# Hybrid encoder layer: side work stepped on every second step, attention as a pipeline of one burst each, all values in front

## The chip, the cores and the metric

One NeuronCore of a Trainium2 chip runs the whole program. The metric is device microseconds from start to end of one execution; the number for a kernel is the median of its runs.

## The reference

One step of a hybrid encoder trunk with one layer, for 512 prompt tokens and 8 sequences of 16 new tokens each, side by side as T = 640 columns. Model width is 2048, all in fp32. Cut to what matters:

```
z = x @ w_in              # q,k,v,f,gate of FoX | q,k,v,a,beta,gate of the delta rule | two merge gates
# branch A, 8 heads: forgetting attention
p = softmax(q k^T * scale + c_q - c_k, causal);  o_a = p @ v      # c: running sum of log-forget
#   prompt: 4 blocks of 128 queries; decode: 16 new queries per sequence over 512 cached rows and themselves
y_a = (o_a * silu(gate_a)) @ w_out_fox
# branch B, 8 heads: gated delta rule
q,k,v = silu(conv4(qkv));  q,k normalised
for chunk n:  v_new = u - w S;  o = q S + (q k^T * decay) v_new;  S = S * g + k_tail^T v_new
y_b = (rms_norm(o) * silu(gate_b)) @ w_out_gdn
h  = (sig(m_a) * y_a + sig(m_b) * y_b) @ w_out
x1 = LayerNorm(alpha * x + h);  out = x1 + sig(x1 @ w_pl_gate) * RMSNorm(p @ w_pl_proj)
```

Keys, values, log-forgets, the conv's last rows and the delta states are outputs too.

## The kernel before, in words

**Main work.** Every fp32 operand of the large products is split into two halves, high and low, and each product is three matmuls (hi·hi, hi·lo, lo·hi). x stays in SBUF as 16 tiles of 128 x 640 and the weights stream through. A *column* is one output block of 128 features: 16 steps, each of six matmuls 128x320 (`mm6`, L303 to L308; a step is thus "six column matmuls"). `pair` (L360 to L401) makes two columns with fewer products (L382). `wide` (L336 to L358) makes the 1024 values of FoX in two groups of 512 features: five row tiles, each a PSUM bank of 512, all five fed by 16 steps (L351). Its five banks are four of tag "g" and one of tag "o". When a row tile is done, `fin` in `values` copies its bank to a temporary in SBUF (ScalarE for even tiles, VectorE for odd) and sends it out by two DMAs: to `vd`, from where the heads read it back, and to the output `out_fv`. There are two temporaries, used in turn, so a copy waits for the two DMAs of the copy before last.

**Stages.** `front` runs the first FoX columns, values group 0 with a sum of x tiles (`sums`) beside it, then 14 pairs. `phase_fox` runs the q and k columns of heads 1 to 7, values group 1 behind head 3, then three merge-gate columns (`mcol`) and two projections. `phase_gdn` runs four columns for each of 8 delta heads (in the order q, k, v, gate) with a merge-gate column behind each, then the output columns. `tail` ends the layer.

**Side work.** Attention and delta rule are generators on *lanes*. After each step of a column, `tick` (L108) lets each lane take one stage of its generator if its wake time has come and, unless the lane is marked dry, if `banks_free` says that the PSUM banks of the next stages will have been read (by a running estimate of costs, `watch`, `clock` and `busy`). What a stage gives to TensorE stands in its queue between two steps of the column; I call it a *burst*. `par` (L129) takes two generators together, the decode part `fox_dec` and the prompt part `fox_pro`. The engines run in program order, so a burst whose input is late holds up the columns behind it. Side work takes PSUM banks from `sps`, tag "s", three banks in the FoX phase and four in the delta phase.

**One FoX head** (`fox`, L575). Prompt, for each block i of queries: scores (`mm3`, L299 to L301; block 0 is one fp32 matmul) into a bank, VectorE adds bias and mask, softmax (max L566, exp L568, scale L570 and L571), transposes of the probabilities (L704, one for each 128 keys), a copy to SBUF (`pT`, ScalarE, L706), output matmuls (L713) and a product with the gate (`og`, L715). Scores of block i+1, transposes of i and output of i are separate bursts. Decode: scores against the cache by 8 matmuls on quarter arrays, 128x32, 512 columns wide (L616) into bank `s1`, its softmax over 640 in `xd`, five transposes (L638, L645), copies `ppad` (L640) and `pn`, then 32 quarter-array matmuls of 128 columns against the cached values (L659) into bank `od`, in four bursts of 8; then a transpose and the store of `og`. A head's k and v caches (four pieces each, 512 KB), its values (`vn`, read back from `vd`) and its bias are loaded by SyncE's DMA queue, which the weight pieces (`wr`) share.

**Weights.** `w_ahead` (L257) issues one load ahead; a piece is then cast to its high half (`wh`, ScalarE, L253) and the low half is the difference (`wl`, VectorE, L254).

Of the kernel before, what the change touches and what calls it, by code (L numbers as in the profile page):

```python
# [9 lines left out]
F32 = mybir.dt.float32  # L10
# [4 lines left out]
ALU = mybir.AluOpType  # L15
# [32 lines left out]
class Kernel:  # L48
# [9 lines left out]
    PAIR0, PAIRS = 6, 4 + FRONT // 2  # L58
# [4 lines left out]
    def __init__(self, tc, ins, outs):  # L63
        self.clock, self.busy, self.paced = 0.0, [0.0, 0.0], False
        self.tc, self.nc, self.i, self.o = tc, tc.nc, ins, outs
        self.lanes = []
        self.banks, self.read, self.nbanks = [], {}, 3
        self.now = 0
# [60 lines left out]
    def par(self, *gens):  # L129

        live = [[g, 0, 0.0] for g in gens]
        t = 0
        while live:
            for e in list(live):
                if e[1] <= t and e[2] <= self.clock:
                    try:
                        n, e[2] = self.watch(e[0])
                        e[1] = t + n
                    except StopIteration:
                        live.remove(e)  # L140
            if live:
                yield self.FREE
                t += 1
# [398 lines left out]
    def values_of(self, h):  # L542

        while self.vdone <= h // 4:
            yield 1
        if h not in self.vn:
            self.vn[h], self.vat = self.zt([P, 5, P], "vn", 2), self.now
            self.nc.sync.dma_start(out=self.vn[h], in_=self.vd[:, :, h * P:(h + 1) * P].rearrange("t p d -> p t d"))
            return
        while self.now < self.vat + 6:  # L550
            yield 1
# [9 lines left out]
    def softmax(self, xs, n):  # L561


        nc = self.nc
        nm = self.zt([P, 1], "nm", 3)
        nc.vector.reduce_max(out=nm, in_=xs[:, 0:n], axis=AX.X, negate=True)  # L566
        sm = self.zt([P, 1], "sm", 3)
        nc.scalar.activation(xs[:, 0:n], xs[:, 0:n], AF.Exp, bias=nm, accum_out=sm)  # L568
        yield 2
        nc.vector.reciprocal(sm, sm)  # L570
        nc.vector.tensor_scalar(out=xs[:, 0:n], in0=xs[:, 0:n], scalar1=sm, scalar2=0.5, op0=ALU.mult,  # L571
                                op1=ALU.mult)
        yield 1
# [35 lines left out]
    def fox_dec(self, h, q, k, sg, og):  # L609
        nc = self.nc  # L610
        nb, nbd = self.bias[h]
        s1 = self.sps()
# [19 lines left out]
        yield 1  # L632
# [10 lines left out]
        yield 1  # L643
# [4 lines left out]
        yield 2  # L648
        yield from self.values_of(h)
        yield from self.values_of(h)  # L650
        vn = self.vn[h]
        od = self.sps()
        nc.tensor.matmul(od[:, 0:P], pn, vn[:, 4, :], start=True, stop=False, skip_group_check=True)
        for par in range(2):
            for c in range(4):
# [5 lines left out]
                if c == 1:  # L661
                    yield
# [4 lines left out]
        on = self.zt([P, P], "sq", 2, "on")  # L667
        nc.scalar.copy(out=on, in_=od[:, 0:P])
        yield 2
# [3 lines left out]
        pt = self.sps()  # L673
        nc.tensor.transpose(pt[:, 0:P], on, self.ident)
        nc.vector.tensor_tensor(out=og[:, NPT:T], in0=pt[:, 0:P], in1=sg[:, NPT:T], op=ALU.mult)
        yield 2

    def fox_pro(self, h, q, k, qp, kp, sg, og):
# [16 lines left out]
        xs = scores(0)  # L695
        yield 2
        for i in range(4):
            w = P * (i + 1)
            yield from self.softmax(xs, w)
            nx = scores(i + 1) if i < 3 else None  # L700
            yield 2
            pt = self.sps()
            for kb in range(i + 1):
                nc.tensor.transpose(pt[:, kb * P:(kb + 1) * P], xs[:, kb * P:(kb + 1) * P], self.ident)  # L704
            pT = self.zt([P, NPT], "pT")
            nc.scalar.copy(out=pT[:, 0:w], in_=pt[:, 0:w])  # L706
            yield 2
            yield from self.values_of(h)
            yield from self.values_of(h)
# [5 lines left out]
            nc.vector.tensor_tensor(out=og[:, i * P:w], in0=ops[:, 0:P], in1=sg[:, i * P:w], op=ALU.mult)  # L715
            xs = nx
# [54 lines left out]
    def gdn(self, h, kq, v):  # L771
# [5 lines left out]
        junk = self.zt([P, P], "junk")  # L777
        kt = self.zt([P, 5, P], "kt", 2)
        vr = self.zt([P, 5, P], "vr", 2)
        pk = self.sps()  # L780
        for t in range(4):
            nc.tensor.transpose(pk[:, t * P:(t + 1) * P], kq[:, 0, t * P:(t + 1) * P], self.ident)
        nc.scalar.copy(out=kt[:, 0:4, :], in_=pk.rearrange("p (a b) -> p a b", b=P))
        yield
        pd = self.sps()
        nc.tensor.transpose(pd[:, 0:P], kq[:, 0, NPT:T], self.ident)
        nc.tensor.transpose(pd[:, P:2 * P], v[:, NPT:T], self.ident)
        nc.tensor.transpose(pd[:, 2 * P:3 * P], kq[:, 1, NPT:T], self.ident)
        nc.scalar.copy(out=kt[:, 4, :], in_=pd[:, 0:P])
        nc.scalar.copy(out=vr[:, 4, :], in_=pd[:, P:2 * P])  # L790
        nc.scalar.activation(junk, pd[:, 2 * P:3 * P], AF.Square, accum_out=ss[:, 9:10])
        yield
        for t in range(5):
            nc.scalar.activation(junk, kt[:, t, :], AF.Square, accum_out=ss[:, t:t + 1])
        yield
        pq = self.sps()
        for t in range(4):
            nc.tensor.transpose(pq[:, t * P:(t + 1) * P], kq[:, 1, t * P:(t + 1) * P], self.ident)
        for t in range(4):
            nc.scalar.activation(junk, pq[:, t * P:(t + 1) * P], AF.Square, accum_out=ss[:, 5 + t:6 + t])  # L800
        yield
        pv = self.sps()
        for t in range(4):
            nc.tensor.transpose(pv[:, t * P:(t + 1) * P], v[:, t * P:(t + 1) * P], self.ident)
        nc.scalar.copy(out=vr[:, 0:4, :], in_=pv.rearrange("p (a b) -> p a b", b=P))
# [278 lines left out]
    def run(self, ctx):  # L1084
# [25 lines left out]
        self.blocks, self.chunks = self.lane(), self.lane()  # L1110
# [19 lines left out]
    def values(self, g, temp, after=None):  # L1130
# [11 lines left out]
        self.wide([self.gps(512) for _ in range(4)] + [self.ps2.tile([P, 512], F32, tag="o", name="o", bufs=1)],  # L1142
                  fin, after)
        self.vdone = g + 1

    def front(self, work):
# [4 lines left out]
        self.vdone = 0  # L1151
# [20 lines left out]
        wu = self.ps2.tile([P, 512], F32, tag="o", name="wu", bufs=1)  # L1172
# [70 lines left out]
        self.values(0, lambda t: self.spare[t % 2], lambda s: sums(s // 2) if s % 2 else None)  # L1243
# [46 lines left out]
    def phase_fox(self, work):  # L1290
# [5 lines left out]
        self.foxdone = -1  # L1296
# [6 lines left out]
        for h in range(H):  # L1303
# [16 lines left out]
            if h == 3:  # L1320
                self.values(1, lambda t: self.zt([P, T], ("sc", "eacc")[t % 2], 1, "vt"))
# [33 lines left out]
    def phase_gdn(self, conv, work):  # L1355
# [13 lines left out]
        for h in range(H):  # L1369
            for c in range(4):  # L1370
                acc = self.column()[0]
                kq = self.kqs[h % 2]
                if c == 2:
                    v = self.zt([P, T], "v")
                self.until(lambda: self.untapped == 0)
                if c == 3:
                    sg = self.zt([P, T], "sg")
                    self.silu_evac(acc, sg, "cth")
                    nc.sync.dma_start(out=self.sgd[h], in_=sg)
                else:  # L1380
                    ct = 8 * c + h
                    self.untapped += 1
                    stp = self.strip_evac(acc, ct)
                    conv["gens"].append(self.conv_silu(stp, ct, h if c == 1 else 0, v if c == 2 else kq[:, 1 - c, :]))
# [68 lines left out]
    def e_evac(self, n, ps):  # L1453

        nc = self.nc
        if n == 0:
            self.until(lambda: not self.work["gens"])
# [280 lines left out]
def _layout(a):  # L1738
# [15 lines left out]
    bl += [bq[0], bk[0], *bv[0]]  # L1754
# [3 lines left out]
    for h in range(1, H):  # L1758
        bl += [bq[h], bk[h], *(bv[1] if h == 3 else [])]
# [4 lines left out]
    for h in range(H):  # L1764
        bl += [gq[h], gk[h], gv[h], gg[h]]
        if h < 7:
            bl += m[nf + 3 + r * h:nf + 3 + r * (h + 1)]
# [72 lines left out]
```

## Time and profile before

| | us |
| --- | --- |
| median of 3 runs | 2252.88 (2249.75 to 2255.94) |
| the profiled execution | 2256.83 |
| its span | 2255.0 |

The profiled execution lies 3.95 us above the median, and 1.8 us of its time lie around the span. TensorE is busy 99% of the span. Rows of the timeline give start, duration, engine, line and operation; in brackets is the idle time of the engine ahead of the row and what ended it. Several equal instructions in a row are one row; a matmul of fp32 shows as two records, so "x16" on such a row is 8 matmuls. The recorded duration of a matmul overlaps the next one's, so costs on TensorE are taken from starts.

### The profile page before, as it was taken

Reading aid. Unit: us, or ns where it says so; the run is one execution under the profiler, and the core shown is the slowest. Engines: PE = TensorE matmul, PEld = TensorE weight load, DVE = VectorE, ACT = ScalarE, POOL = GpSimd, SP = SyncE. Lnnn points to the kernel's source line nnn. Section 1 sums busy time; section 2 is a strip of 40 time slices with the busy share of each in tenths; the row PEclk is TensorE's granted clock in tenths of the full one; section 3 lists DMA queues with packets and bytes.
Section 4 is the critical chain, followed back from the end, with each engine's and each line's share of the span. In section 5 each row is a group of like instructions: output and inputs, shape, how many; then the busy total and the mean of one; then the engine's idle time right before and its main releaser. Section 6 shows DMA issues by size and latency. Waiting matters only on the chain.

```text
span 2255.0 us, 39956 instructions
## 1 busy us (share of the span) xinstructions
PE 2240.8 (99%) x15938; PEld 2154.1 (96%) x15938; DVE 1328.8 (59%) x2831; ACT 842.7 (37%) x1874; POOL 68.3 (3%) x230
## 2 busy tenths in 40 slices
PE   9999999999999999999999999999999999999999
PEld 7899999988799999999999999999999999999999
DVE  5867666633434345476776776776537533667555
ACT  4444443423233335443543543544332212243222
POOL 0000000000000000000001000000000000020000
PEclk9999999999999999999999999999999999999999
DMA  6333332466555555223333323335447532323332
GB/s 226 124 117 104 122 118 99 134 223 212 198 191 191 179 171 172 93 85 101 106 101 101 109 92 98 119 103 174 161 156 234 174 99 99 99 98 108 122 122 69
DMA packets 118378, 304.56 MB, mean 135 GB/s; under 512 B 22680, under 2 KB 30952, under 8 KB 118192
## 3 DMA queue, kind: packets, MB, share of 16 engines
q1 hardware_dynamic: 118192, 302.01, 40.1%
q8 instruction: 125, 2.05, 0.4%
q14 instruction: 61, 0.50, 0.1%
HBM read 250.15 MB, written 51.82 MB: 134 GB/s over the span
## 4 chain that ended last, share of the span: by engine, by line
PE 95%; DVE 2%; DMA 2%; ACT 1%; issue 0%; SPq 0%; ACTq 0%; DVEq 0%
PE g L307 34%; PE g L308 33%; PE g L382 15%; PE g L351 3%; PE s L659 1%; PE s L713 1%; PE s L616 1%; PE o L351 1%; PE s L852 1%; DMA wr<-in_w 0%; PE s L989 0%; PE s L704 0%; DMA kc<-in_kc 0%; DVE wl L254 0%; DVE xr L1231 0%
## 5 line engine op out<-in xcount | busy, mean ns | idle before, releaser
L254 DVE TENSOR_TENSOR wl<-wr,wh 128x512 fp32r<-128x512 f32 x556 | 380.8, 690 | 523.5 <-ACT wh L253 496.9
L307 PE MATMUL g<-xh,wh 128*128 128x320 f32 (+1 forms) x1712 | 555.7, 325 | 0.6 <-ACT wh L253 0.4
L253 ACT CAST wh<-wr 128x512 fp32r<-128x512 f32 x556 | 341.1, 619 | 511.4 <-PE g L308 427.9
L307 PE MATMUL g<-xl,wh 128*128 128x320 f32 (+1 forms) x1712 | 530.0, 310 | 0.3 <-DVE xl L282 0.3
L308 PE MATMUL g<-xh,wh 128*128 128x320 f32 x1712 | 529.6, 309 | 0.0
L307 PE MATMUL g<-xh,wl 128*128 128x320 f32 (+1 forms) x1712 | 529.2, 309 | 0.0
L308 PE MATMUL g<-xl,wh 128*128 128x320 f32 x1712 | 529.1, 309 | 0.0
L308 PE MATMUL g<-xh,wl 128*128 128x320 f32 x1712 | 528.9, 309 | 0.0
L307 PEld LDWEIGHTS g<-xh,wh 128*128 128x128 f32 x1712 | 323.0, 189 | 17.6 <-issue 12.7
L308 PEld LDWEIGHTS g<-xh,wh 128*128 128x128 f32 x1712 | 323.0, 189 | 0.7
L307 PEld LDWEIGHTS g<-xl,wh 128*128 128x128 f32 x1712 | 322.8, 189 | 0.7 <-DVE xl L282 0.7
L308 PEld LDWEIGHTS g<-xl,wh 128*128 128x128 f32 x1712 | 322.6, 188 | 0.0
L307 PEld LDWEIGHTS g<-xh,wl 128*128 128x128 f32 x1712 | 322.0, 188 | 0.1
L308 PEld LDWEIGHTS g<-xh,wl 128*128 128x128 f32 x1712 | 321.8, 188 | 0.0
L382 PE MATMUL g<-xh,wh 128*128 128x320 f32 x448 | 138.6, 309 | 1.1 <-ACT u L392 1.1
L382 PE MATMUL g<-xh,wl 128*128 128x320 f32 x448 | 138.6, 309 | 0.0
L382 PE MATMUL g<-xl,wh 128*128 128x320 f32 x448 | 138.5, 309 | 0.0
L254 DVE TENSOR_TENSOR wl<-sr,wh 128x512 fp32r<-128x512 f32 x112 | 75.7, 690 | 62.3 <-ACT wh L253 62.0
L253 ACT CAST wh<-sr 128x512 fp32r<-128x512 f32 x112 | 67.8, 617 | 68.2 <-PE g L382 68.2
L382 PEld LDWEIGHTS g<-xh,wh 128*128 128x128 f32 x448 | 84.2, 188 | 1.4 <-ACT u L392 1.4
L382 PEld LDWEIGHTS g<-xh,wl 128*128 128x128 f32 x448 | 84.3, 188 | 0.0
L382 PEld LDWEIGHTS g<-xl,wh 128*128 128x128 f32 x448 | 84.1, 188 | 0.0
(388 smaller groups left out, 2921.2 us busy)
## 6 DMA issues: line engine op xcount, KB each, us to landing
wr<-in_w SPq DMA_DIRECT2D x276, 512.0 KB, 3.6
kc<-in_kc SPq DMA_DIRECT2D x32, 512.0 KB, 5.2
vc<-in_vc SPq DMA_DIRECT2D x32, 512.0 KB, 4.1
xr<-in_xT SPq DMA_DIRECT2D x32, 320.0 KB, 3.9
md<-m SPq DMA_DIRECT2D x32, 320.0 KB, 2.5
sab<-md SPq DMA_DIRECT2D x32, 320.0 KB, 3.5
sr<-in_w SPq DMA_DIRECT2D x14, 512.0 KB, 4.4
ed<-e SPq DMA_DIRECT2D x16, 320.0 KB, 3.7
```

Of the source, the lines that this page charges most:

```text
L253: nc.scalar.copy(out=hi, in_=src)
L254: nc.vector.tensor_tensor(out=lo, in0=src, in1=hi.bitcast(F32), op=ALU.subtract)
L307: nc.tensor.matmul(ps[0], whl[w], xhl[o][:, a], start=(first and x == 0), stop=(last and x == 2))
L308: nc.tensor.matmul(ps[1], whl[w], xhl[o][:, b], start=(first and x == 0), stop=(last and x == 2))
L351: nc.tensor.matmul(ps, x[:, sl], w, start=(s == 0 and n == 0), stop=(s == 15 and n == 2))
L382: nc.tensor.matmul(ps, a[:, w], b, start=(k == 0 and n == 0 and not more), stop=(k == 7 and n == 2), skip_group_check=True)
L616: nc.tensor.matmul(s1[32 * j:32 * j + 32, :], self.qpad[:, 2 * j + par, :], kc[:, (j % 2) * NPT:(j % 2 + 1) * NPT], start=(par == 0), stop ...
L659: nc.tensor.matmul(od[32 * j:32 * j + 32, 0:P], self.ppad[:, c, 2 * j + par, :], vc[:, o:o + P], start=False, stop=(par == 1 and c == 3), ...
L713: nc.tensor.matmul(ops[:, 0:P], vn[:, kb, :], pT[:, kb * P:(kb + 1) * P], start=(kb == 0), stop=(kb == i))
L852: nc.tensor.matmul(pp[:, o:o + 256].rearrange("p (a b) -> p a b", a=2), hl[w][:, 0, x], hl[m][:, :, x], start=(n == 0), stop=(n == 2))
```

## The change

Nothing is computed that was not computed before; instructions change places, and banks.

- Lanes that are not dry step on every second tick (`every` = 2; 1 from delta head 7 on). The lane `blocks` is now dry. `par` counts ticks.
- A new bank tag "d" with one bank (`dps`) takes the place of "o"; it holds `s1`, `od` and the wide's fifth row tile.
- Values: both groups run in `front`, one behind the other; `sums` goes with the second. `values_of` is gone: `load_v` reads a head's values back when the head starts.
- `fox_pro` is a pipeline: one burst holds the output of block i-2, the transposes of block i-1 and the scores of block i+1, and softmax i follows. `fox_dec` gives its quarter-array output matmuls in two bursts of 16 in place of four of 8, and its five transposes in one. The bias of the next head is loaded inside `fox_dec`, behind the head's last scores. The last transpose and the store of `og` go to the lane `ends` (`fox_out`).
- Delta rule: order of columns q, v, k, gate; the 15 transposes at a head's start go in two bursts (7 and 8) in place of four.

The diff, cut to its core:

```diff
     def tick(self):
         self.now += 1
         for q in self.lanes:
-            if q["gens"] and q["wake"] <= self.now and q["t"] <= self.clock and (q["dry"] or self.banks_free()):
+            if q["gens"] and q["wake"] <= self.now and q["t"] <= self.clock and (
+                    q["dry"] or not self.paced or (self.now % self.every == 0 and self.banks_free())):
                 self.step(q)
...
+    def dps(self):
+        return self.ps2.tile([P, 512], F32, tag="d", name="s", bufs=1)
...
     def fox(self, h, q, k):
-        if self.vdone > h // 4:
-            yield from self.values_of(h)
+        self.load_v(h)
...
-        og = self.zt([P, T], "og")
-        yield from self.par(self.fox_dec(h, q, k, sg, og), self.fox_pro(h, q, k, qp, kp, sg, og))
-        if h + 1 < H:
-            self.load_bias(h + 1)
-        nc.sync.dma_start(out=self.ogd[h], in_=og)
-        yield
+        yield from self.par(self.fox_dec(h, q, k), self.fox_pro(h, q, k, qp, kp, sg))
+        self.ends["gens"].append(self.fox_out(h, sg))
...
     def fox_dec
-        s1 = self.sps()
+        s1 = self.dps()
...
-        yield 1
         pt = self.sps()
         nc.tensor.transpose(pt[:, 0:P], xd[:, NPT:T], self.ident)
         pn = self.zt([P, P], "sq", 2, "pn")
         nc.scalar.copy(out=pn, in_=pt[:, 0:P])
-        yield 2
-        yield from self.values_of(h)
-        yield from self.values_of(h)
+        yield 4
+        while self.scored < h:
+            yield 2
+        if h + 1 < H:
+            self.load_bias(h + 1)
         vn = self.vn[h]
-        od = self.sps()
+        od = self.dps()
...
                     nc.tensor.matmul(od[32 * j:32 * j + 32, 0:P], ...)
-                if c == 1:
-                    yield
...
     def fox_pro
+        xs, pT, og = [scores(0)], None, None
+        for i in range(5):
+            if i:
+                if i == 2:
+                    while self.outdone < h - 1:
+                        yield 2
+                    self.og = og = self.zt([P, T], "og")
+                if i > 1:
+                    output(i - 2)
+                w = P * i
+                pt = self.sps()
+                for kb in range(i):
+                    nc.tensor.transpose(pt[:, kb * P:(kb + 1) * P], xs[i - 1][:, kb * P:(kb + 1) * P], self.ident)
+                pT = self.zt([P, NPT], "pT")
+                nc.scalar.copy(out=pT[:, 0:w], in_=pt[:, 0:w])
+            if i < 3:
+                xs.append(scores(i + 1))
+            if i == 2:
+                self.scored = h
+            if i < 4:
+                yield from self.softmax(xs[i], P * (i + 1))
+            yield 2
+        output(3)
+        yield 2
...
     def front
-        self.values(0, lambda t: self.spare[t % 2], lambda s: sums(s // 2) if s % 2 else None)
+        for g in range(2):
+            self.values(g, lambda t: self.spare[t % 2], lambda s: sums(s // 2) if g and s % 2 else None)
...
     def phase_gdn
+            if h == 7:
+                self.every = 1
```

**TensorE, output matmuls of decode.** These rows are TensorE's queue in a middle head (`vc` are the cached values, `ppad` the spread probabilities, `g` a column's bank). Before:

```order
L653 MATMUL s<-vn,pn 128x128
L659 MATMUL s<-vc,ppad 32x128 x8
L307 MATMUL g<-xh,wh 128x320
L308 MATMUL g<-xh,wh 128x320
L307 MATMUL g<-xl,wh 128x320
L308 MATMUL g<-xl,wh 128x320
L307 MATMUL g<-xh,wl 128x320
L308 MATMUL g<-xh,wl 128x320
L659 MATMUL s<-vc,ppad 32x128 x8
```

After, in the same place:

```order
L313 MATMUL g<-xh,wl 128x320
L647 MATMUL s<-vn,pn 128x128
L653 MATMUL s<-vc,ppad 32x128 x16
L699 MATMUL s<-pT,vn 128x128 x3
L715 MATMUL s<-cb,xs 128x128 x4
L312 MATMUL g<-xh,wh 128x320
```

Sixteen quarter-array matmuls now stand in one piece, and the prompt's output of block 2 and the transposes of block 3 stand right behind them.

**TensorE, the two bursts with scores and transposes of decode.** Here the buffer numbers are shown, and the semaphores on which a row waits. Before, in head 3 (L638 transposes `xd`, L299 to L301 are scores, L351 are the values between them):

```order
L638 MATMUL s_6036<-cb_287,xd_5970 128x128 [waits DVE_49,PE_49]
L638 MATMUL s_6036<-cb_287,xd_5970 128x128 x3
L299 MATMUL s_6043<-kh_5874,qh_5870 128x384
L300 MATMUL s_6043<-kl_5875,qh_5870 128x384
L301 MATMUL s_6043<-kh_5874,ql_5871 128x384
L351 MATMUL g_5914<-wh_5854,xh_257 128x512
L351 MATMUL g_5914<-wh_5854,xl_258 128x512
L351 MATMUL g_5914<-wl_5855,xh_257 128x512
L645 MATMUL s_6053<-cb_287,xd_5970 128x128
```

After, the burst with the decode scores' second half and the prompt's last scores:

```order
L609 MATMUL s_5740<-kc_5777,qpad_5078 32x512
L616 MATMUL s_5844<-k_5087,q_5086 128x128
L699 MATMUL s_5851<-pT_5795,vn_5710 128x128 [waits DMAHW0_49,Activation_49]
L715 MATMUL s_5854<-cb_287,xs_5754 128x128 [waits DVE_49]
L715 MATMUL s_5854<-cb_287,xs_5754 128x128
L304 MATMUL s_5859<-kh_5718,qh_5714 128x512 [waits Activation_49]
L305 MATMUL s_5859<-kl_5719,qh_5714 128x512
L306 MATMUL s_5859<-kh_5718,ql_5715 128x512
```

and, 36 column matmuls on, the burst with the transposes of `xd`:

```order
L631 MATMUL s_5935<-cb_287,xd_5846 128x128 [waits DVE_49]
L631 MATMUL s_5935<-cb_287,xd_5846 128x128 x3
L637 MATMUL s_5942<-cb_287,xd_5846 128x128
L699 MATMUL s_5946<-pT_5857,vn_5710 128x128 x2
L715 MATMUL s_5950<-cb_287,xs_5801 128x128 [waits DVE_49,PE_49,Activation_49]
L715 MATMUL s_5950<-cb_287,xs_5801 128x128 x2
```

Four groups stand in one burst. s_5859 lies in the same PSUM bank as s_5854 (three "s" banks), so L304 waits for the ScalarE copy (L717) that reads the transposes issued just ahead of it in the same burst; s_5950 lies in the bank of s_5935, so L715 waits for the two `ppad` copies (L633) of the transposes at the burst's head. In the order of before, no burst takes a bank twice.

**SyncE, the loads ahead of the first FoX head.** `nb` and `nbd` are the bias, `kc` and `vc` the caches, `wr` weight pieces. Before:

```order
L1308 DMA q<-qkd_152 128x640
L1308 DMA k<-qkd_153 128x640
L555 DMA nb<-rd 128x640
L557 DMA nbd<-sfd 128x1x512
L539 DMA kc<-in_kc 128x1024 x3
L223 DMA wr<-in_w 128x1024
L539 DMA vc<-in_vc 128x1024 x3
L586 DMA sg<-sgf_144 128x640
L548 DMA vn<-vd 128x5x128
L223 DMA wr<-in_w 128x1024 x3
L539 DMA kc<-in_kc 128x1024
```

After:

```order
L1313 DMA q<-qkd_152 128x640
L1313 DMA k<-qkd_153 128x640
L228 DMA wr<-in_w 128x1024
L554 DMA nb<-rd 128x640
L556 DMA nbd<-sfd 128x1x512
L544 DMA kc<-in_kc 128x1024 x3
L544 DMA vc<-in_vc 128x1024 x3
L228 DMA wr<-in_w 128x1024
L584 DMA sg<-sgf_144 128x640
L550 DMA vn<-vd 128x5x128
L228 DMA wr<-in_w 128x1024 x2
L544 DMA kc<-in_kc 128x1024
```

The first weight piece moves ahead of the bias and the six cache pieces, the second ahead of the gate and the values.

More of the change, by code (lines that the diff above doesn't have):

```diff
@@ L540, in load_kv, with load_v @@
         store[h, j] = a
-    def values_of(self, h):
-        while self.vdone <= h // 4:
-            yield 1
[L546 to L551, printed above, removed]
+    def load_v(self, h):
+        self.vn[h] = self.zt([P, 5, P], "vn", 2)
+        self.nc.sync.dma_start(out=self.vn[h], in_=self.vd[:, :, h * P:(h + 1) * P].rearrange("t p d -> p t d"))
     def load_bias(self, h):
@@ L666, in fox_dec @@
                 yield 6
[L667 to L669 removed]
+        self.on = self.zt([P, P], "sq", 2, "on")
+        nc.scalar.copy(out=self.on, in_=od[:, 0:P])
         if h + 1 < H:
@@ L693, in scores, with output @@
             return xs
[L695 to L709, printed above, removed]
+        xs, pT, og = [scores(0)], None, None
+        def output(i):
             vn = self.vn[h]
@@ L1109, in run @@
         work, conv, self.ends = self.lane(), self.lane(True), self.lane()
-        self.blocks, self.chunks = self.lane(), self.lane()
+        self.blocks, self.chunks = self.lane(True), self.lane()
         self.work = work
@@ L1141, in fin @@
             nc.sync.dma_start(out=self.o["fv"][t][:, g * 512:(g + 1) * 512], in_=x)
-        self.wide([self.gps(512) for _ in range(4)] + [self.ps2.tile([P, 512], F32, tag="o", name="o", bufs=1)],
+        self.wide([self.gps(512) for _ in range(4)] + [self.dps()],
                   fin, after)
-        self.vdone = g + 1
     def front(self, work):
@@ L1372, in phase_gdn @@
                 kq = self.kqs[h % 2]
-                if c == 2:
+                if c == 1:
                     v = self.zt([P, T], "v")
-                self.until(lambda: self.untapped == 0)
                 if c == 3:
+                    self.until(lambda: not conv["gens"])
                     sg = self.zt([P, T], "sg")
@@ L1456, in e_evac @@
         if n == 0:
-            self.until(lambda: not self.work["gens"])
+            self.until(lambda: not self.work["gens"] and not self.ends["gens"])
             self.eacc = self.zt([P, T], "eacc")
```

79 lines of the change are left out of this document (38 added, 41 removed).

## The prediction

> **What bounds the kernel now.** I read the page first: the span, the busy shares and the chain that ended last.
>
> ```profile
> span 2255.0 us, 39956 instructions
> PE 2240.8 (99%) x15938; PEld 2154.1 (96%) x15938; DVE 1328.8 (59%) x2831; ACT 842.7 (37%) x1874; POOL 68.3 (3%) x230
> PE 95%; DVE 2%; DMA 2%; ACT 1%; issue 0%; SPq 0%; ACTq 0%; DVEq 0%
> ```
>
> TensorE is busy 99% of the span and 95% of the chain is its own. A change that keeps every matmul can gain in three ways only: TensorE's waits go, matmuls cost less where they now stand, or the clock drops less. How much the first can bring is in the waits of TensorE by releaser (total, times, longest):
>
> ```profile
> PE s L704 <- DVE xs L571: 3.8, 1, 3.8
> PE s L1512 <- DVE rym L1506: 1.6, 1, 1.6
> PE g L382 <- ACT u L392: 1.1, 1, 1.1
> PE s L1020 <- ACT xx L1016: 0.5, 1, 0.5
> ```
>
> Attention and delta rule together (L704, L1020) make TensorE wait 4.3 us, nearly all in one place. What stands closer together after the change can only lengthen this list. So the question is how much cheaper bursts get, and how many new waits that costs.
>
> **What a burst costs.** In the timeline, a burst of plain matmuls (four transposes, then two fp32 matmuls of 128x128) between columns:
>
> ```profile
> 490.21 0.31 PE L308 MATMUL g<-xh,wh 128*128 128x320 f32 x1
> ...
> 490.79 0.31 PE L308 MATMUL g<-xh,wl 128*128 128x320 f32 x1
> 490.94 0.60 PE L638 MATMUL s<-cb,xd 128*128 128x128 f32 x4
> 491.37 0.61 PE L713 MATMUL s<-pT,vn 128*128 128x128 f32 x4
> 491.74 0.40 PE L307 MATMUL g<-xh,wh 128*128 128x320 f32 x1
> 491.97 0.31 PE L308 MATMUL g<-xh,wh 128*128 128x320 f32 x1
> ```
>
> Between the first two rows lie four column matmuls in 0.58 us, 0.146 each. From 490.79 to 491.97 are 1.18; less two columns the burst cost 0.89. The transposes take 0.43 (0.11 each), which leaves 0.22 for a plain fp32 matmul. And a burst of 8 quarter-array matmuls:
>
> ```profile
> 497.01 0.31 PE L308 MATMUL g<-xh,wl 128*128 128x320 f32 x1
> 497.25 0.65 PE L659 MATMUL s<-vc,ppad 128*32 128x128 f32 x16
> 497.83 0.41 PE L307 MATMUL g<-xh,wh 128*128 128x320 f32 x1
> 498.08 0.31 PE L308 MATMUL g<-xh,wh 128*128 128x320 f32 x1
> ```
>
> Here 1.07 less 0.29 leaves 0.78. Four stand side by side, so they stream as two plain ones, 0.44. The other **0.34 us** is paid for going into the quarter-array shape and out of it; I take it as paid once for a burst, however long.
>
> The Trainium skill has the rule in "TensorEngine Tiling (Array Packing)", section Key Properties: a change of tiling mode drains TensorE. The rows agree with 0.34; the page gives no time.
>
> **The change part by part.**
>
> *1. Fewer bursts.* In the order, side work stands in 354 pieces between column matmuls before and in 245 after. Of the 109 that go, 16 are quarter-array bursts of `od` (four become two in each of 8 heads): 16 x 0.34 = −5.4. In the delta heads 7 more pieces of such small shapes come to stand directly against another; each saves between nothing and 0.34, I take half: −1.2. The other 86 are plain; the rows above leave no more than 0.01 for each: −0.5. Together **−7.1** (bounds −5 and −8.5).
>
> *2. A wait inside a burst, twice in each FoX head.* In the order after, L304 stands right behind two transposes whose bank it takes, and waits until ScalarE has copied them; one burst on, L715 waits for the two `ppad` copies. No row of before has this; its parts are here:
>
> ```profile
> 488.96 0.38 PE L704 MATMUL s<-cb,xs 128*128 128x128 f32 x2
> 489.47 0.36 ACT L706 COPY pT<-s 128x256 f32<-128x256 f32 x1
> 491.63 0.65 ACT L640 COPY ppad<-s 128x256 f32<-128x256 f32 x2 [1.80 <-PE s L638]
> 477.41 0.28 DVE L571 TENSOR_SCALAR xs<-xs,sm 128x128 f32<-128x128 f32 x1
> 477.76 0.47 PE L704 MATMUL s<-cb,xs 128*128 128x128 f32 x1 [3.76 <-DVE xs L571]
> ```
>
> The last of the four transposes quoted above starts at 491.27 and the waiting ScalarE starts at 491.63: 0.36. From an end on VectorE (477.69) to the released matmul are 0.07. First wait: 0.36 + 0.36 for the copy + 0.07, less 0.11 that the transpose takes anyway: 0.68. Second: 0.36 + 0.65 + 0.07 behind the fourth transpose, less the 0.11 + 0.11 + 2 x 0.22 that stand between: 0.42. So 1.1 a head, **+8.8** for 8 heads. Nothing hides it: TensorE takes its queue in order, and behind the waiting matmul stand the columns. Bounds: +6 if the copies start at half that delay; +18 if in each wait a weight cast (0.6 us, L253) stands ahead on ScalarE.
>
> *3. Values behind values.* Group 1 now starts on group 0's banks at once. ScalarE's copies at the end of group 0, and TensorE's rate in the group (records in 30 us):
>
> ```profile
> 96.38 0.56 ACT L1139 COPY sa<-g 128x512 f32<-128x512 f32 x1
> 99.76 0.59 ACT L1139 COPY sa<-g 128x512 f32<-128x512 f32 x1 [2.82 <-DMA out_fv<-sa]
> 103.29 0.59 ACT L1139 COPY sa<-o 128x512 f32<-128x512 f32 x1 [2.94 <-DMA out_fv<-sa]
> 60.00:90.00 30.00, 29.45 (x127) 23.22 (x126) 1.00 0.30 93
> ```
>
> 30 / 127 is 0.236 a matmul, so a row tile's three take 0.71. Tile 0 is done 0.36 ahead of its copy, at 96.0; tile 4, and with it the group, at 96.0 + 4 x 0.71 = 98.85. Group 1 then wants tile 4's bank at 98.85 + 2.84 = 101.7. But its copy waits for the DMAs of tile 2's copy, out of the same temporary, and ends at 103.88, released at 103.95: **+2.3**. The copies of tiles 1 and 3 on VectorE come sooner (the sums are now in the second group) and can at best be on time; nothing shortens ScalarE's. Bounds 0 (if the DMAs land in half the time) and 3. At the end of group 1 the 1.1 of L382 stays.
>
> *4. Softmax of decode.* Its transposes (L631) stand 36 column matmuls (36 x 0.146 = 5.3 us) behind the burst with the scores. VectorE and ScalarE rows (count: shortest/median/longest ns) and the low half of a weight piece:
>
> ```profile
> L626 DVE SCALAR_TENSOR_TENSOR xd<-nbd,colT,s x8: 746/748/750, 481.8 to 811.9; 128x512 f32<-128x512 f32 x8
> L566 DVE TENSOR_REDUCE nm<-xd x8: 808/810/814, 487.3 to 814.3; 128x1 f32<-128x640 f32 x8
> L568 ACT ACTIVATE xd<-xd,nm x8: 830/831/833, 488.1 to 815.1; 128x640 f32<-128x640 f32 x8
> L571 DVE TENSOR_SCALAR xd<-xd,sm x8: 553/554/556, 489.5 to 816.3; 128x640 f32<-128x640 f32 x8
> L254 DVE TENSOR_TENSOR wl<-wr,wh 128x512 fp32r<-128x512 f32 x556 | 380.8, 690 | 523.5 <-ACT wh L253 496.9
> ```
>
> From the last matmul of `s1` to the columns the burst takes 3 x 0.22 + 2 x 0.11 less the overlap + 0.68 + three 512-wide fp32r matmuls (about 0.24 each, from part 3) = 2.1, so 7.4 are there. VectorE can do little of the prompt's block ahead of the burst's end; behind it come bias (0.75) and mask (0.28) of block 3, the maximum of block 2 (about 0.5) and of `xd` (0.81), then exp (0.83 + 0.2), reciprocal and scale (0.16 + 0.55): 2.1 + 0.4 + 2.3 + 1.0 + 0.7 = 6.5, and one or two low halves in the same queue (0.69 each) make 7.2 to 7.9. So between nothing and 1.5 a head; I take 0.5: **+4** (bounds 0 and +12). In the trace of before the same transposes hardly ever wait.
>
> *5. Delta rule.* A chain of twelve column matmuls (1.75 us) from link to link stays; it waited once for 0.5 (L1020). The lane `blocks` is now dry and runs its VectorE work (0.3 to 0.4 an operation) beside it, a conv's operation and a low half (0.69) may fall in with it. One place in each of 8 heads at 0 to 0.9; I take 0.3: **+2.5** (bounds 0 and +7).
>
> *6. The first FoX head.* The windows of the trace there (busy and counts of five engines, clock, DMA share, GB/s), and ScalarE's row:
>
> ```profile
> 475.12 0.62 ACT L253 CAST wh<-wr 128x512 fp32r<-128x512 f32 x1 [7.54 <-DMA wr<-in_w]
> 464.00:470.00 6.00, 6.00 (x44) 4.97 (x43) 1.88 (x4) 1.14 (x2) 0.59 (x1) 1.00 1.04 394
> 470.00:476.00 6.00, 3.99 (x28) 3.73 (x27) 0.23 (x1) 0.62 (x1) 0.00 (x0) 1.00 0.91 350
> 476.00:482.00 6.00, 4.24 (x16) 2.25 (x17) 2.60 (x8) 1.27 (x4) 0.11 (x1) 0.58 0.31 100
> 482.00:488.00 6.00, 6.00 (x37) 6.00 (x37) 3.05 (x7) 1.76 (x5) 0.12 (x1) 0.85 0.17 55
> ```
>
> The DMA engines are full, a weight piece lands late, the softmax queues behind its cast, TensorE idles 3.76 and then runs at a lowered clock: (1 − 0.58) x 6 + (1 − 0.85) x 6 = 3.4. Together 7.2. After, the order has one weight piece ahead of all caches and the next ahead of gate and values, so the late one lands some 640 KB earlier, 1.6 us at 394 GB/s. But the bytes are the same, and more VectorE work stands ahead of the scale. If all goes: −7.2; if the wait only turns up elsewhere: 0. I take the 1.6 and little of the clock: **−2**.
>
> The DMAs of moved steps (bias one stage earlier, `vn` at the head's start, `og` one step later) and the denser stream of caches in the FoX stage I cost at nothing: a cache piece takes these times to land (median us), six steps or 5.3 us are kept for it, and the next pieces are ahead by more.
>
> ```profile
> kc<-in_kc SPq DMA_DIRECT2D x32, 512.0 KB, 5.2
> vc<-in_vc SPq DMA_DIRECT2D x32, 512.0 KB, 4.1
> ```
>
> Without that cover a late piece costs up to 1 us a head; the upper end allows for it.
>
> **The sum.** −7.1 + 8.8 + 2.3 + 4 + 2.5 − 2 = +8.5 on the profiled execution's own 2256.8: 2265.3. The median of the runs lies 3.95 under that execution, so I put the time at **2261**. From all lower bounds (−8.5 + 6 + 0 + 0 + 0 − 7.2 = −9.7) to all upper ones (−5 + 18 + 3 + 12 + 7 + 0 = +35) is far too wide to be met together; it is the frame of the range.
>
> **Rivals.**
>
> *A. A changeover at every burst: faster.* The first column behind a burst starts 0.23 to 0.25 before the second, not 0.146. I counted that excess (0.085) to the matmuls of the burst. If it belongs to the return to columns, each of 109 bursts less saves it: −9.3. It decides if a long plain burst is cheaper than its parts; the quoted one, 0.89 for 4 x 0.11 + 2 x 0.22, speaks against it. With the softmax of part 4 on time as well: 2261 − 9.3 − 4 − 5 (the clock at the first head kept up) = 2243.
>
> *B. The first head is mended and the chains fit.* −7.2 in place of −2, parts 4 and 5 at nothing: 2261 − 5.2 − 6.5 = 2249. For it: waits of before are few. Against: less room and more in each burst.
>
> *C. The chains do not fit.* VectorE does a second low half ahead of the scale in each head, and both in-burst waits meet a cast: parts 4 and 5 at their upper bounds, 2261 + 8 + 4.5 = 2273.
>
> *D. The clock drops in every FoX head.* If the new waits lowered it as at the first head: 8 x 3.4 more, 2288. Against it: around the wait of 1.6 (L1512, at 1695.7) the clock stayed full,
>
> ```profile
> 1694.00:1704.00 10.00, 8.39 (x54) 8.01 (x54) 9.83 (x18) 2.87 (x6) 0.00 (x0) 1.00 0.63 211
> ```
>
> only 3.76 lowered it, and no wait that I expect passes 2.3.
>
> The Trainium skill has a rule each way in "TensorE: Matmul & The Clock Gate": its section HAM oscillation names gaps above about 3.4 us, with which the trace agrees (3.76 did, 1.6 did not), and its section A second HAM failure mode says that small idles from cycling through PSUM banks can do it too, which no row here shows.
>
> **How the numbers follow.** A measurement of this kernel can tell about 0.3%, 6.8 us, from no change: 2246.1 to 2259.6. The forecast (2254 to 2268) has a chance of 0.48, with a third of it under 2259.6; A 0.14, B 0.18, C 0.17, D 0.03. Faster: A, 0.14. Within 0.3%: B and a third of the forecast, 0.34. Slower: two thirds of the forecast, C and D, 0.52. The range leaves out most of A, the upper half of C and D: 2246 to 2274.
>
> **What would show it.** Right: L304 and L715 wait for ScalarE's `pT` and `ppad` in the list of TensorE's waits, eight times each, 0.5 to 0.8 and 0.3 to 0.5; L351 waits once, some 2 us, for the copy of the fifth bank; 16 bursts of quarter-array output matmuls cost 1.2 each where 32 cost 0.78; L631 waits in some heads. Wrong: no wait at L304 (then part 2 falls and the time is near 2252), a burst of plain matmuls that costs less than its parts (A), a lowered clock in several FoX heads (D), or a wait of several us for a cache piece.

## The result and the profile after

| | before | after |
| --- | --- | --- |
| median, us | 2253.39 (2249.75 to 2255.94) | 2270.81 (2269.83 to 2271.93) |
| profiled execution | 2256.83 | 2269.83 |
| its span | 2255.0 | 2268.0 |

The ratio is 1.0079 (95% interval 1.0061 to 1.0096): the change makes the kernel slower by 0.8%. In a later series of runs it was 1.0075 (1.0061 to 1.0089). One execution of experiment 10, at 3097.79 us and a granted clock of 0.654, was in a slow state and counts in no ratio.

The page after, its first lines:

```profile
span 2268.0 us, 39946 instructions
PE 2238.6 (99%) x15938; PEld 2154.2 (95%) x15938; DVE 1330.1 (59%) x2831; ACT 841.0 (37%) x1874; POOL 69.3 (3%) x230
```

TensorE is busy 2.2 us less in a span 13 us longer. So nothing became slower on TensorE itself: it waits. The list of its waits, after (engine, tile and line, what ended the wait; total us, times, longest):

```profile
PE s L1059 <- DVE S L1077: 5.5, 6, 1.2
PE s L631 <- DVE xd L570: 4.4, 5, 1.4
PE s L304 <- ACT pT L717: 4.1, 8, 0.5
PE s L715 <- DVE xs L570: 3.5, 2, 2.9
PE s L715 <- ACT ppad L633: 1.5, 8, 0.2
PE wu L1178 <- DVE z L1175: 1.2, 1, 1.2
PE s L356 <- ACT sa L1145: 1.2, 1, 1.2
PE g L387 <- ACT u L397: 1.1, 1, 1.1
PE g L312 <- ACT xh L286: 0.6, 1, 0.6
PE g L356 <- DVE sb L1143: 0.5, 1, 0.5
```

Of before's waits over 1 us the start (L1178), the pairs (L387) and the first head's softmax (L704, now L715) are left; L1512's 1.6 is gone. Five kinds of waits stand in front that were not there or stood once. Two of them come eight times each, once a head, with the same length: the sign of a wait that the order makes, not one of chance.

**The wait inside a burst.** Timeline of TensorE in the third FoX head, from the last column matmul ahead of the burst:

```profile
618.80 0.31 PE L313 MATMUL g<-xh,wl 128*128 128x320 f32 x1
619.04 1.06 PE L609 MATMUL s<-kc,qpad 128*32 128x512 f32 x8
620.03 0.49 PE L616 MATMUL s<-k,q 128*128 128x128 f32 x2
620.36 0.39 PE L699 MATMUL s<-pT,vn 128*128 128x128 f32 x2
620.58 0.38 PE L715 MATMUL s<-cb,xs 128*128 128x128 f32 x2
621.48 0.50 PE L304 MATMUL s<-kh,qh 128*128 128x512 f32 x1 [0.52 <-ACT pT L717]
621.82 0.40 PE L305 MATMUL s<-kl,qh 128*128 128x512 f32 x1
622.05 0.40 PE L306 MATMUL s<-kh,ql 128*128 128x512 f32 x1
622.29 0.31 PE L312 MATMUL g<-xh,wh 128*128 128x320 f32 x1
```

and ScalarE there:

```profile
621.06 0.37 ACT L717 COPY pT<-s 128x256 f32<-128x256 f32 x1 [3.02 <-PE s L715]
```

The two transposes start at 620.58 and would be followed at 620.80. L304 starts at 621.48, 0.05 behind the end of the copy: 0.68 late. And it needs 0.34 until L305 follows, where L305 and L306 need 0.23 and 0.24: TensorE loses another 0.1 as it starts again (in experiment 1, where L304 does not wait, L305 follows it by 0.22 to 0.24). By its starts the burst costs 3.33 us, its parts 2.52: 0.81 more.

The second such wait, one burst on in the same head:

```profile
628.31 0.66 PE L631 MATMUL s<-cb,xd 128*128 128x128 f32 x4 [0.56 <-DVE xd L570]
628.80 0.27 PE L637 MATMUL s<-cb,xd 128*128 128x128 f32 x1
628.91 0.61 PE L699 MATMUL s<-pT,vn 128*128 128x128 f32 x4
629.70 0.55 PE L715 MATMUL s<-cb,xs 128*128 128x128 f32 x3 [0.18 <-ACT ppad L633]
```

The two fp32 matmuls of L699 (four records) take 0.22 each, so L715 could start at 629.35; it starts at 629.70. In the heads where L631 does not wait, this burst costs 0.58 more than its parts.

**The output matmuls of decode**, 16 on quarter arrays in one piece (32 records), in the next burst but one:

```profile
633.61 0.38 PE L647 MATMUL s<-vn,pn 128*128 128x128 f32 x2
633.93 1.08 PE L653 MATMUL s<-vc,ppad 128*32 128x128 f32 x32
634.94 0.94 PE L699 MATMUL s<-pT,vn 128*128 128x128 f32 x6
```

1.01 from start to start where before 8 took 0.58: twice the matmuls, 0.43 more, the streaming of two plain ones. The part paid once was not paid twice.

**The delta rule.** VectorE's queue where L1059 waits for `S` (L1077), and TensorE:

```profile
1080.92 0.37 DVE L889 TENSOR_TENSOR sx<-sx,lanes 80x184 f32<-80x184 f32 x1
1081.33 0.34 DVE L891 TENSOR_TENSOR sx<-sx,sx 80x184 f32<-80x184 f32 x1
1081.70 0.34 DVE L889 TENSOR_TENSOR sx<-sx,lanes 80x176 f32<-80x176 f32 x1
1082.08 0.34 DVE L891 TENSOR_TENSOR sx<-sx,sx 80x176 f32<-80x176 f32 x1
1082.34 0.90 DVE L761 SCALAR_TENSOR_TENSOR cy<-strip,taps,cy 128x664 f32<-128x664 f32 x1
1083.16 0.34 DVE L1077 SCALAR_TENSOR_TENSOR S<-S,gl,s 128x128 f32<-128x128 f32 x1
1083.55 0.49 PE L1059 MATMUL s<-S,kq 128*128 128x128 f32 x2 [0.87 <-DVE S L1077]
```

`S` stands behind four operations of the blocks (`sx`) and one of the conv (`cy`), 2.2 us of VectorE's work without a gap, and is 0.87 late.

**The first head and the clock.** The windows around its wait (busy and counts of five engines, clock, DMA share, GB/s):

```profile
524.00:530.00 6.00, 6.00 (x44) 4.97 (x43) 0.00 (x0) 0.00 (x0) 0.24 (x1) 1.00 1.04 397
530.00:536.00 6.00, 3.14 (x22) 2.88 (x21) 3.14 (x9) 1.79 (x5) 0.00 (x0) 1.00 0.78 295
536.00:542.00 6.00, 5.68 (x40) 4.41 (x38) 3.62 (x10) 2.09 (x7) 0.24 (x1) 1.00 0.41 144
```

The DMA engines are as full as before and TensorE idles 2.9 us in place of 3.8, but the clock stays at 1.00 where it fell to 0.58. By the Trainium skill ("TensorE: Matmul & The Clock Gate", section HAM oscillation) gaps above about 3.4 us do it; these two idles lie on either side of that, but experiment 8's trace does not agree: its idle of 2.4 us is followed by a clock of 0.72. So the length of the idle alone does not decide; the last section says what the traces show of it.

### The profile page after: what moved, and what is told of

It is laid out like the page before. It is cut to its first block, busy times and chain, and to the rows that moved or that the text cites. A ratio compares the mean times of both kernels' runs of the same rounds, so it can differ in the third digit from the quotient of the medians.

```text
span 2268.0 us, 39946 instructions
## 1 busy us (share of the span) xinstructions
PE 2238.6 (99%) x15938; PEld 2154.2 (95%) x15938; DVE 1330.1 (59%) x2831; ACT 841.0 (37%) x1874; POOL 69.3 (3%) x230
## 5 line engine op out<-in xcount | busy, mean ns | idle before, releaser
L312 PE MATMUL g<-xh,wh 128*128 128x320 f32 (+1 forms) x1712 | 547.5, 320 | 1.0 <-ACT xh L286 0.6
L387 PE MATMUL g<-xh,wh 128*128 128x320 f32 x448 | 138.6, 309 | 1.1 <-ACT u L397 1.1
L387 PE MATMUL g<-xh,wl 128*128 128x320 f32 x448 | 138.6, 309 | 0.0
L387 PE MATMUL g<-xl,wh 128*128 128x320 f32 x448 | 138.5, 309 | 0.0
L387 PEld LDWEIGHTS g<-xh,wh 128*128 128x128 f32 x448 | 84.2, 188 | 1.4 <-ACT u L397 1.4
L387 PEld LDWEIGHTS g<-xh,wl 128*128 128x128 f32 x448 | 84.3, 188 | 0.0
L387 PEld LDWEIGHTS g<-xl,wh 128*128 128x128 f32 x448 | 84.1, 188 | 0.0
```

What stands on the lines that cost most here:

```text
L312: nc.tensor.matmul(ps[0], whl[w], xhl[o][:, a], start=(first and x == 0), stop=(last and x == 2))
L387: nc.tensor.matmul(ps, a[:, w], b, start=(k == 0 and n == 0 and not more), stop=(k == 7 and n == 2), skip_group_check=True)
```

## The experiments

Times are medians, with the ratio to the kernel before on the same chip.

**1. The last scores in a burst of their own.**

```diff
+            if i == 2:
+                yield 2
             if i < 3:
                 xs.append(scores(i + 1))
```

> The changed kernel with one line more: in each FoX head the last scores (L304) come one stage later, in a burst of their own, so that they no longer stand behind the transposes whose bank they take. Theory (the wait inside the burst): the burst with L304 costs 3.33 us by its starts where its parts are worth 2.52, 0.81 x 8 heads; that goes, 6.5 us under the changed kernel, near 2264, and L304 leaves the list of waits. Rival (the head is bound by the chain of its softmaxes, and the wait only shows where the chain is late): the scores of block 3 come 12 columns later, the waits of L631 and L715 grow by as much, and the time stays at 2271.

2260.91, ratio 1.0039 (1.0024 to 1.0054). The waits:

```profile
PE s L1061 <- DVE S L1079: 5.5, 6, 1.2
PE s L631 <- DVE xd L570: 3.7, 4, 1.4
PE s L715 <- DVE xs L570: 3.0, 2, 2.4
PE s L715 <- ACT ppad L633: 1.5, 8, 0.2
```

L304 is gone from the list, and the waits of L631 and L715 did not grow by 6.5, as the rival wanted: L631's fell from 4.4 to 3.7, and L715's 3.0 lies between the 3.5 and the 1.9 of the changed kernel's two profiled executions. (Lines behind the edit move down by two.) The gain is larger than the 6.5 expected: the time is 7.8 under that of the changed kernel when it ran again (experiment 5), the span 7.0.

**2. The decode transposes one slot later.**

```diff
         yield from self.softmax(xd, T)
-        yield 2
+        yield 4
```

> The changed kernel with the decode transposes (L631) one slot of two steps later behind the softmax over 640. Theory (VectorE has too little time between the scores and the transposes): L631's waits (4.4 us in the list, 4.9 by starts, in five of eight heads) go, 5 us under the changed kernel, near 2266; the wait of L715 for the ppad copies stays if both still share a burst. Rival (VectorE's queue is what bounds the head): the wait turns up at the next thing that needs VectorE, L715, and the time stays within 2 us of 2271.

2262.93, ratio 1.0045 (1.0029 to 1.0062), 5.8 under experiment 5 where 5 were expected. From the list of waits:

```profile
PE s L304 <- ACT pT L717: 4.1, 8, 0.5
PE s L715 <- DVE xs L570: 1.7, 1, 1.7
PE s L715 <- ACT ppad L633: 1.5, 8, 0.2
```

L631 left it (4.4 before the edit), L715's wait for its softmax did not grow, and ppad's stayed at 1.5 as the burst is still shared. A place with room takes the wait away; VectorE's queue is late there, not full.

**3. Four temporaries for the values.**

```diff
+        m = tf("m1"), tf("m2")
         for g in range(2):
-            self.values(g, lambda t: self.spare[t % 2], ...)
+            self.values(g, lambda t: (*self.spare, *m)[t % 4], ...)
-        m = tf("m1"), tf("m2")
```

> The changed kernel with four temporaries in place of two for the values on their way out (the two further ones are tiles that are allocated a little later anyway). Theory (the second group waits for the copies, and the copies for the DMAs out of the same temporary): L356's two waits (0.5 and 1.2 us) go, 1.7 to 2.7 us under the changed kernel, near 2268.5. Rival (the DMAs are late because the queues are full there): the copies wait as long, no difference.

2264.25, ratio 1.0051 (1.0036 to 1.0066). Both L356 rows are gone, and with them L387's 1.1, which I had not named: it went with the same edit. From the first matmul of the values to the last of the pairs the trace takes 3.8 us less than in experiment 5, more than the 1.7 to 2.7 expected. So the waits were for the temporary, not for full queues. The pairs waited as long in the kernel before (L382, 1.1); this edit was not run on it.

**4. Lanes on every step.**

```diff
-        self.lanes, self.every = [], 2
+        self.lanes, self.every = [], 1
```

> The changed kernel with lanes stepped on every step again, in place of every second. Theory 1 (the coarse steps put the delta rule's links 12 columns apart just behind VectorE's other work): the six waits of L1059 for S (5.5 us in the list, 7.1 by starts) go or shrink, up to 7 us under the changed kernel, near 2264; the FoX waits inside bursts stay. Theory 2 (they come from the lane that is now dry): L1059 waits as before and some quarter-array pieces part again, 2271 to 2273.

2263.94, ratio 1.0049 (1.0034 to 1.0064). The waits:

```profile
PE s L715 <- DVE xs L570: 7.0, 7, 4.7
PE s L304 <- ACT pT L717: 4.1, 8, 0.5
PE s L1059 <- DVE S L1077: 0.8, 1, 0.8
```

Five of the six waits for `S` went, and L631's and ppad's too; L715's softmax waits more instead. Its longest wait, 4.7 in the first head, is followed by 6.8 us at a granted clock of 0.50, which costs 3.4 more; so the time is only 4.8 under experiment 5. L304 stayed to a tenth: it does not depend on when bursts come, only on what stands in one.

**5. The changed kernel again.**

> The changed kernel unchanged, beside the others on the same chip, since the four experiments so far lie 1 to 4 us lower than their terms account for. If chips or jobs differ: about 2267 to 2269 here. If the terms are too small: 2271 again.

2268.72, ratio 1.0075 (1.0061 to 1.0089). 2.1 us under its first median. In its list of waits one row over 1 us is another:

```profile
PE s L715 <- DVE xs L570: 1.9, 2, 1.3
```

The first head's wait is 1.3 in place of 2.9, most of what the two spans differ by (2265.9 and 2268.0). So up to 2 us of what experiments 1 to 4 gained beyond their terms is the difference between two series of runs.

**6. The blocks' lane not dry.**

```diff
-        self.blocks, self.chunks = self.lane(True), self.lane()
+        self.blocks, self.chunks = self.lane(), self.lane()
```

> The changed kernel with the lane of the delta rule's blocks not dry, as before the change; steps stay every second. With the steps on every step L1059's waits nearly went. Theory 1 (the coarse grid is their cause, whatever the lane): L1059 waits still, some 5 us, time as the changed kernel. Theory 2 (the blocks' VectorE work ahead of S, which the dry lane lets in, is the cause and the grid only sets where): L1059's waits go, other waits of the delta rule may come, and the small pieces part again (six pieces at about 0.2 more): 3 to 6 us under the changed kernel.

2266.24, ratio 1.0062 (1.0046 to 1.0077), 2.5 under experiment 5 where 3 to 6 were expected. L1059 leaves the list; a wait of L1067 for `rp` (1.3, three times) takes a part of it, and three pieces part again, so that the bursts of the delta rule together cost 3.9 less by starts, not the 7.1 that the waits for `S` had cost. With 4: either edit alone ends the wait. It takes both, a grid that puts the link 12 columns behind its state and VectorE work that may come at any step.

**7. All four edits (1 to 4) together.**

> The four edits together: last scores one stage later, decode transposes one slot later, four temporaries, lanes on every step. Theory (each wait has a cause of its own): 6.5 (L304) + 4.9 (L631) + 4.0 (L356 and the wait of the pairs behind) + 6.3 (L1059) + up to 4.6 (L715 for ppad, if the decode transposes come to stand alone) less 1.5 for pieces that part: 24 to 26 us under the changed kernel, 2244 to 2248, under the kernel before. Rival (VectorE's queue bounds the heads, so waits only move): the waits of L715 for its softmax grow as in the run with every step (7.0), 2252 to 2256, no better than before.

2249.90, ratio 0.9987 (0.9978 to 0.9995): 18.8 under the changed kernel beside it, and just under before. Expected were 24 to 26. The list names most of the rest:

```profile
PE s L715 <- DVE xs L570: 4.4, 1, 4.4
PE s L1061 <- DVE S L1079: 0.8, 1, 0.8
```

L304, L631, L356 and ppad are gone, the last because the decode transposes now stand alone. What is left is once, in the first head, 4.4, and behind it the clock is lowered (window 530 to 536; the clock is the third number from the end), 0.50 for 3.4 us by the trace:

```profile
530.00:536.00 6.00, 5.68 (x32) 5.49 (x36) 2.62 (x7) 1.38 (x4) 0.00 (x0) 0.74 0.10 27
```

**8. Before, with the output matmuls of decode in two bursts.**

```diff
-                if c == 1:
-                    yield
```

> The kernel before with one part of the change alone: the output matmuls of decode in two bursts of 16 in place of four of 8. Theory (0.34 us for each quarter-array burst): 16 bursts less, 5.4 us under the kernel before, 2247.5, and each longer burst costs 1.2 where each shorter one cost 0.78. Rival (the time belongs to each matmul on a quarter array and not to the burst): each longer burst costs 1.55 and the time stays within 1 us of before.

2250.06, ratio 0.9989 (0.9980 to 0.9998). By starts each longer burst costs 1.21 (1.19 to 1.21 in the eight heads) against 2 x 0.78: 16 times 0.34 is saved, 5.5 us, and the rival (1.55) falls. But the time fell by 2.4 only: two new waits took some of it (L672 for `on` 1.5, L711 for `pT` 0.7). Even this small merge paid a part of its gain back in waits. The first head's wait (L702) is 2.4 here, and the window behind it has a lowered clock:

```profile
476.00:482.00 6.00, 5.85 (x31) 3.85 (x32) 3.23 (x9) 0.36 (x2) 0.24 (x1) 0.72 0.31 93
```

**9. All four, and the first head's value caches loaded one at a time.**

```diff
-            yield 3
-            for j in range(3):
-                self.load_kv(0, "v", j)
-            yield 3
+            yield 6
...
-        yield (16 if h == 0 else 1)
+        for j in range(3 if h == 0 else 0):
+            yield 5
+            self.load_kv(0, "v", j)
+        yield 1
```

> The run with all four edits and one more: the first head's three value-cache pieces are loaded one at a time, five steps apart, in place of all three at once ahead of two weight pieces. Theory (the loads of the first head delay a weight piece, ScalarE's cast of it, and with it the softmax): the wait of L715 (4.4 in the list; the burst costs 6.17 where its parts are 0.63) goes, 5.5 us under the run with all four, 2244.4. Rival (the bytes are the same, the DMA engines full for 18 us, so another weight piece is late): 2 to 4 us of wait at another place, 2248 to 2250.

2245.58, ratio 0.9969 (0.9959 to 0.9980), 4.3 under experiment 7 where 5.5 were expected. L715's wait fell from 4.4 to 0.3, and the list of waits is nearly empty; beside the 1.2 at the start its longest are:

```profile
PE s L1061 <- DVE S L1079: 0.8, 1, 0.8
PE s L609 <- DMA kc<-in_kc: 0.8, 1, 0.8
```

This is the fastest version, 7 us under before.

**10. Before, with the same spread.**

> The kernel before with the same edit alone. Theory: its wait of 3.76 at L704 and the lowered clock behind it (3.4 by the windows) go: 2249 if the runs of before lose the wait alone, 2245.5 if they lose both. Rival (same bytes): L704 waits as before or another instruction does, 2252.5.

2251.19, ratio 0.9995 (0.9986 to 1.0004): no difference that can be told, as the rival had it. L704's wait fell from 3.8 to 0.2, but L616 now waits for a cache piece:

```profile
PE s L616 <- DMA kc<-in_kc: 1.4, 1, 1.4
...
PE s L704 <- DVE xs L571: 0.2, 1, 0.2
```
Its profiled execution (2251.54) lies at its median. The profiled execution of before lost 7 us at this place; its other runs cannot have lost as much, or the edit would have shown more than 1.5.

## Why the prediction was right, and where its terms were off

The way, slower, and the mechanism were right, and the time is in the range; it is 10 us over the forecast, a rise of 17.4 where 8.1 was forecast. Measured by starts on both profiled executions (a burst's cost is the time from the column matmul ahead of it to those behind, less the columns):

| term | predicted | measured |
| --- | --- | --- |
| fewer bursts | −7.1 | −8.4 |
| waits inside a burst | +8.8 | +11.1 |
| values behind values | +2.3 | +2.7 |
| softmax of decode (L631) | +4 | +4.9 |
| delta rule (L1059) | +2.5 | +7.1 |
| first head, and softmax waits of L715 | −2 | −2.6 |
| L1512 | none | −1.9 |
| sum | +8.5 | +12.9 |

The two executions lie 13.0 apart. All bursts together cost 231.8 before and 241.8 after; without the waits and the lowered clock in them (9.2 and 27.6) 222.6 and 214.2: that is the first row.

*1. Fewer bursts:* right. The 0.34 is paid once for a burst (experiment 8), as the Trainium skill's rule of the drain ("TensorEngine Tiling (Array Packing)", section Key Properties) has it; no page gives the 0.34. Rival A, a changeover at each plain burst as well, would have made this row −16; it fell.

*2. Waits inside a burst:* right, a fourth too small. L304 came 0.68 late, as predicted; the 0.1 of a new start was left out, and with it the first wait costs 0.81. The second costs 0.58, not 0.42; the list, which counts only the idle time, shows 0.2 of it, less than the 0.3 to 0.5 named as the sign. Experiment 1 shows the first; that the second goes when the two stand apart is seen in experiment 7.

*3. Values:* right (2.3 against 2.7, experiment 3); the fifth bank's copy is waited for 1.2 in the list and not 2, and another 0.5 is for a copy of VectorE's (`sb`).

*4. Softmax of decode:* right; five heads wait, 0.56 to 1.4, three do not.

*5. Delta rule: the term that was mis-sized.* I priced one place a head at 0.3, between nothing and 0.9. It is one place in six heads, at 1.14 each by starts, once 1.42. The upper bound 0.9 was the wait itself (0.87 in the list); again the new start costs more. And the value was taken low because before's links of 12 columns hardly wait. But the two edits that meet there (grid and dry lane) both changed what stands ahead of `S`. Taking the wait out did not give 7.1 back: the delta rule's bursts became 4.3 shorter in experiment 4 and 3.9 in experiment 6, as pieces that the change had joined part again or wait elsewhere.

*6. First head:* within the bounds, but near the forecast by luck. The wait shrank by 0.9 and not by 1.6, the clock kept all of its 3.4, and later waits of L715 took some 1.7 back. That an idle of 2.9 left the clock up was chance too: experiment 8's 2.4 did not.

*The step from the profiled execution to the median failed.* I took off 3.95, as if before's profiled execution lay above its median for a reason that the changed kernel shares. The changed kernel's profiled execution lies 1.0 under its median. Before's 3.95 is about what the lowered clock cost there (3.4), and neither profiled execution of the changed kernel has such a stretch. Experiment 10 fits, and the mean granted clocks of the other runs support it. The profiled execution of before shows 0.998 and a span of 2255.0. Of the 46 executions of before that ran beside the experiments, 14 show 1.000 (median span 2249.6), 28 show 0.999 (2251.2) and only 4 show 0.998 (2252.6). A stretch of 6.8 us at 0.50 alone makes 0.998, so most of them did not have it. It is not before's alone, though: one of the four executions in experiment 5, 2272.95 and the longest, shows 0.998 as well. With this step left out, the forecast would have been 2265.3, and the miss 5.5 us, of which the delta rule makes 4.6.

Rival B (first head mended, chains on time) and C (chains at their upper bounds, 2273) each had a part: C's time was nearest, by the delta rule and not by the softmax or the in-burst waits that it named with it: that is luck. D, a clock that drops in every head, did not happen: the waits behind the first head are 0.2 to 1.4, and the clock is 1.00 there. But my ground against it, that only 3.76 lowered the clock, was weak: experiment 8's 2.4 did too.

## What to carry to other kernels

When TensorE is 99% busy and takes its queue in order, merging bursts saves only what a burst pays for itself: here 0.34 us where it goes into quarter-array shape, next to nothing for plain matmuls. Every merge must be read for what now stands directly behind its own producer: a bank that is taken twice within a burst costs a trip through ScalarE (here 0.81 and 0.58 us), each time. The savings of this change were there (8.4 us), and with the new waits taken out one by one it became a gain (0.9969), though two of the waits taken out, the pairs' and the first head's, stood in the kernel before as well. And a profiled execution should be compared with its own median before any term is carried from one to the other.

## What the runs showed of the hardware

A wait costs TensorE more than its length: behind 0.87 of waiting (L1059) the burst is 1.14 longer, behind L304's wait the first matmul takes 0.34 to the next start in place of 0.23. An idle of 2.9 us (the changed kernel) left the clock at 1.00; idles of 2.4 (experiment 8), 3.8 (before) and 4.4 (experiment 7) were followed by windows at 0.72, 0.58 and 0.74.

The traces show more. The granted clock is 1.00 or 0.50 (a window's 0.72 is a mean), and in each of the twelve traces its changes lie a whole number of steps of 3.413 us apart (in before, 471.04 us, 138 steps, lie between the first change and the drop). Counted in these steps, TensorE's idle time tells the cases apart. Five steps with 1.72 us idle (experiment 2, during the values), 2.43 (experiment 8), 2.95 (before) and 3.41 (experiments 4 and 7) are each followed by one or two steps at 0.50. No step at full clock with 1.66 us idle or less is. In the changed kernel the edge of a step cuts the 2.9 into 1.66 and 1.20, in experiment 8 the 2.4 falls into one step; so it is a matter of chance whether a wait of this size costs the clock.
